# Attention in a hybrid decoder layer: three visits of TensorE per head pair instead of eight short ones

## The chip, the cores and the metric

The kernel runs on one core of a Trainium2 chip. A core has a matrix engine, TensorE (PE in the profile, with its weight loads listed apart as PEld), and three engines for elementwise work: VectorE (DVE), ScalarE (ACT) and GpSimd (POOL). SyncE (SP) issues the transfers here. All of them run their own instruction lists and meet at semaphores. The metric is device time in microseconds (us) from the start to the end of one execution; the time of a kernel is the median of its runs.

## The reference

One decoder layer on 512 tokens of width 1024, in fp32. Three sub-layers follow one another, each behind an RMS norm that is scaled and shifted by a conditioning vector:

```
x += 0.5 * (1 + ga1) * swiglu(norm1(x))          # 1024 -> 2816 -> 1024
x += (1 + ga2) * mixer(norm2(x))
x += 0.5 * (1 + ga3) * swiglu(norm3(x))
mixer: q, k, v of 16 heads of 64 = h @ w_in;  out = heads @ w_o
  8 stick-breaking heads, keys before the query only:
    z = q.k / 8;  w = sigmoid(z) * product over the keys between key and query of sigmoid(-z)
  8 forgetting heads, keys up to the query:
    q, k RMS-normed per head;  p = softmax(q.k / 8 + F[query] - F[key]),  F = running sum of log sigmoid(f)
  out = weights @ v
```

## The kernel before

**Precision and tiles.** A fp32 product is made as three matmuls of split operands: high part by high part, high by low, low by high (`mm3`, lines 127 to 130). Tokens lie along the free axis, 512 wide, so that a projection of 128 output columns is eight steps (one for each 128 of the width 1024), each of three 128x512 matmuls. A weight tile is loaded by a transfer of SP into `raw`; ACT copies it to the high part `hi` (line 123) and DVE, or the engine that `prep` (line 120) is given, subtracts that to get the low part `lo` (line 124). The accumulators are PSUM banks with four tags (line 107): three banks `mm`, two `z`, two `pt`, one `o`.

**The mixer.** The heads are taken in pairs, in `ORDER`: pairs 4 to 7 are the forgetting heads (the code says fox), 0 to 3 the stick-breaking ones. The tokens are stored last first, so that block i of 128 queries sees the last 512 - 128 i columns. For each pair `project` (line 756) makes q and k. For a fox pair the accumulator goes through `norm_start` (line 770: squares `nsq`, their high part `nsh`, on POOL the low part `nsl`) and `norm_end` (line 776: two matmuls against a block of ones into an `mm` bank, the reciprocal root `nr`, the normed `nq`). `q_stack` and `k_stack` then split the normed q and k into stacked operands: `QH`, `QL`, `KS` and, for fox, `late` (shown as `k` in the profile). These pieces wait in the list `side`, and one of them is popped for each projection step.

A unit is a pair and one block of queries, 32 in all. It has three parts on PE:

- `scores` (line 830): for each head a matmul of `QH` by `KS`, and a second one with `QL` (64 rows only for stick-breaking), into `z`; for fox a bf16 matmul adds the mask. Behind it `weigh` works on the other engines. Fox: the row maximum `mx` on DVE, exp to `fw` with the row sum `sm` on ACT, the reciprocal on DVE, the scaling of `fw` on POOL. Stick-breaking: two sigmoids `keep` and `beta` on ACT, a scan to `R` on DVE, `beta` times `R` on POOL.
- `transposed` (line 879), for each head: 4 - i transposes of the weights into `pt`, then a copy `PT` on DVE or ACT.
- `values` (line 890): the products with `V` (PV), 128*64, into `o`; after the pair's last unit `heads_out` splits `o` into `oh` and `ol`.

**The order on PE** in the mixer is written out by hand. `filler` (line 936) yields projection steps: q and k of the pairs, two of the four chunks of `V`, then the output projection for three of its eight tiles as far as its inputs are there. `advance(n)` (line 968) issues such steps up to number n. The main loop (from line 976) goes over the units and puts, for unit u: its scores, steps, the transposes of unit u - 1's first head, a step, the PV of unit u - 2, steps, the transposes of unit u - 1's second head, steps. How many steps come between is set by `target(t)` (line 656), where t counts half units: 2.5 steps for each until t = 52, from there 1.125. After the last step the rest of the output projection follows.

The other engines' orders are made by a scheduler from dependencies and priorities; the weights of the attention have a priority raised by 200 (line 848). An engine takes its list strictly in order.

Of the kernel before, what the change touches and what calls it, by code (L numbers as in the profile page):

```python
# [15 lines left out]
P = 128  # L16
# [17 lines left out]
def hybrid_layer(  # L34
# [47 lines left out]
    def nm(s):  # L82
        uid[0] += 1
        return f"{s}_{uid[0]}"
# [513 lines left out]
    SIDE = 1  # L598

    V = mp.tile([P, 4, D], F32, tag="V", name="V")  # L600
    fcol = mp.tile([P, 8, 8], F32, tag="fcol", name="fcol")[:, :4, :]
    evn = [0]

    def evac(dst, src):
# [66 lines left out]
    free_sb = mconst([P, S], BF16, "free_sb")  # L671
    keep_sb = mconst([P, S], BF16, "keep_sb")
    nc.gpsimd.memset(free_sb, 0.0)
    nc.gpsimd.affine_select(
        out=free_sb[:, :P], in_=free_sb[:, :P], compare_op=ALU.is_gt, fill=1.0, base=0, pattern=[[1, P]],
        channel_multiplier=-1,
    )
    nc.gpsimd.memset(keep_sb, 1.0)
    nc.gpsimd.affine_select(
        out=keep_sb[:, :P], in_=keep_sb[:, :P], compare_op=ALU.is_gt, fill=0.0, base=0, pattern=[[-1, P]],  # L680
        channel_multiplier=1,
    )
# [4 lines left out]
    logf = mp.tile([P, 8, 8], F32, tag="logf", name="logf")[:, :4, :]  # L687
# [68 lines left out]
    def project(p, got):  # L756
        fox = p >= NPAIR
        for u in range(2):
            wt = prep(wqk[2 * p + u], D, nc.gpsimd if fox and u else None)
            b = bank("mm")  # L760
            for k in range(KD):
                lh, ll = wk(wt, k)
                mm3(b, lh, ll, h["h"][k], h["l"][k], k == 0, k == KD - 1)
                if k == KD - 1:
                    got.append(norm_start(b) if fox else b)
                yield
# [60 lines left out]
            ]  # L827
        )

    def scores(p, i):  # L830
        while p not in ready:
            side.pop(0)()
        KS, QH, QL = ST[p]
        fox = p >= NPAIR
        n = S - i * P
        nn = max(n, 256)
        zs = [bank("z") for _ in range(2)]
        qsl, ksl = slice(i * P, (i + 1) * P), slice(S - nn, S)
        for g, z in enumerate(zs):
            nc.tensor.matmul(z[:, :nn], QH[:, g, qsl], KS[:, g, ksl], start=True, stop=False)  # L840
            if fox:
                nc.tensor.matmul(z[:, :nn], QL[:, g, qsl], late[p % 2][:, g, ksl], start=False, stop=False)
                nc.tensor.matmul(z[:, nn - n : nn - n + P], ident_b, mask_fx, start=False, stop=True)
# [6 lines left out]
    def weights(p, g, i, z, n):  # L850
        with tc.high_priority(offset=200):
            return weigh(p, g, i, z, n)

    def weigh(p, g, i, z, n):
        if p >= NPAIR:
            hd = 2 * (p - NPAIR) + g
            mx = mp.tile([P, 1], F32, tag="mx", name=nm("mx"), bufs=4)
            sm = mp.tile([P, 1], F32, tag="sm", name=nm("sm"), bufs=4)
            lq = lfq[:, i, hd : hd + 1]
            nc.vector.tensor_reduce(mx, z, AX.X, ALU.max)  # L860
            nc.vector.scalar_tensor_tensor(
                out=mx, in0=mx, scalar=lq, in1=lq, op0=ALU.add, op1=ALU.subtract, reverse1=True
            )
            w = wt2k("fw")
            act(w[:, :n], z, AF.Exp, bias=mx, accum_out=sm)
            nc.vector.reciprocal(sm, sm)
            nc.gpsimd.tensor_scalar(w[:, :n], w[:, :n], sm, 0.0, op0=ALU.mult, op1=ALU.add)
            return w, n
# [4 lines left out]
        rti[0] += 1  # L873
        nc.vector.tensor_tensor_scan(
            R[:, 1:n], keep[:, : n - 1], free_sb[:, : n - 1], 1.0, op0=ALU.mult, op1=ALU.max
        )
        nc.gpsimd.tensor_tensor(beta[:, :n], beta[:, :n], R[:, :n], op=ALU.mult)
        return beta, n

    def transposed(p, g, w, n):  # L880
        pt = bank("pt")
        for j in range(n // P):
            nc.tensor.transpose(pt[:, j * P : (j + 1) * P], w[:, j * P : (j + 1) * P], ident)  # L883
        PT = mp.tile([P, S], F32, tag="PT", name=nm("PT"), bufs=4)
        if p < NPAIR:
            nc.vector.tensor_tensor(PT[:, :n], pt[:, :n], keep_sb[:, :n], op=ALU.mult)
        elif g:
            nc.scalar.copy(PT[:, :n], pt[:, :n])
        else:
            nc.vector.tensor_copy(PT[:, :n], pt[:, :n])  # L890
        return PT

    def values(p, i, pts, ob):
        n = 4 - i
        for j in range(n):
            for g in range(2):
                nc.tensor.matmul(  # L897
                    ob[g * 64 : g * 64 + 64, i * P : (i + 1) * P],
                    V[:, i + j, (2 * p + g) * 64 : (2 * p + g + 1) * 64],
                    pts[g][:, j * P : (j + 1) * P],  # L900
                    start=j == 0,
                    stop=j == n - 1,
                )

    def heads_out(p, ob):
        if p in ORDER[-2:]:
# [66 lines left out]
            if side and done[0] % SIDE == 0:  # L973
                side.pop(0)()

    units = [(p, i) for p in ORDER for i in range(4)]
    with tc.manual_schedule(engines={ENG.PE}):
        advance(36)
        ws, pts, obs = {}, {}, {}
        for u in range(len(units) + 3):  # L980
            if u < len(units):
                ws[u] = scores(*units[u])
            for g in range(2):
                advance(target(2 * u + g))
# [12 lines left out]
        acc = SumSq(tmps(mp, "wk", NWK))

# [111 lines left out]
```

## Time and profile before

| | before |
|---|---|
| median of 3 runs | 1024.78 us (1024.21 to 1025.28) |
| profiled execution | 1024.78 us, of which the span from the first to the last instruction is 1023.0 us |
| mean granted TensorE clock | 0.998 |
| busy in the span | PE 1004.3, PEld 832.3, DVE 577.4, ACT 372.0, POOL 125.3 us |
| window 410 to 450 us, where attention starts | PE busy 34.64 of 40 us, clock 0.96 |
| window 450 to 620 us, the rest of attention | PE busy 167.15 of 170 us, DVE 130.67, ACT 105.08, POOL 68.80 |
| window 700 to 1023 us, the last sub-layer | PE busy 319.47 of 323 us |

The profile gives each engine's busy time, what its idle time waited for, and a timeline of its instructions. Matmuls overlap in the array and their ends are modelled, so the busy time of PE contains pauses inside a chain of matmuls; the times from start to start show them. In a timeline row stand the start in us, the duration, engine, line, operation, output<-inputs, tile (rows*columns for PE), shapes and the number of instructions. A bracket behind it gives idle time and what ended it.

### The profile page before, as it was taken

The numbers are of one execution on the slowest core, as the hardware profiler recorded it, in microseconds if no ns is written. First come the engines' busy times: TensorE is split into PE (matmuls) and PEld (weight loads), VectorE is DVE, ScalarE is ACT, GpSimd is POOL, SyncE is SP. The second block draws the span as 40 slices with busy tenths as digits, with TensorE's granted clock in tenths as the row PEclk, the third lists the DMA queues.
The fourth block names the chain that finished last, engine by engine and source line by source line (L and its number), as shares of the span: only waits on it lengthen the run. The fifth ranks groups of instructions, "written<-read, shape, count | busy, mean of one in ns | idle before, by whom it ended". The sixth has DMA issues, their size and how long they took to land.

```text
span 1023.0 us, 13213 instructions
## 1 busy us (share of the span) xinstructions
PE 1004.3 (98%) x5164; PEld 832.3 (81%) x5164; DVE 577.4 (56%) x950; ACT 372.0 (36%) x600; POOL 125.3 (12%) x125
## 2 busy tenths in 40 slices
PE   8999999999999999989999999999999999999998
PEld 7788788888888899767787767998888888888887
DVE  6999888524333447699867675753333233333331
ACT  4343212322222335677566461543222222123320
POOL 1000000000000123345313355100000000000000
PEclk9999999999999999999999999999999999999999
DMA  7989899433332312302111112233322222332321
GB/s 299 317 298 327 323 338 334 145 91 101 103 103 86 121 51 79 116 25 68 56 63 62 48 37 62 84 103 103 103 86 100 103 87 81 115 107 86 89 80 57
DMA packets 37358, 128.88 MB, mean 126 GB/s; under 512 B 4400, under 2 KB 4656, under 8 KB 37296
## 3 DMA queue, kind: packets, MB, share of 16 engines
q1 hardware_dynamic: 35712, 125.88, 36.1%
q10 hardware_dynamic: 1584, 2.16, 0.6%
q8 instruction: 41, 0.67, 0.3%
q14 instruction: 21, 0.17, 0.0%
HBM read 125.92 MB, written 2.10 MB: 125 GB/s over the span
## 4 chain that ended last, share of the span: by engine, by line
PE 82%; DVE 9%; issue 3%; DMA 2%; ACT 2%; POOL 1%; SPq 0%; ACTq 0%; DVEq 0%; POOLq 0%
PE mm L128 10%; PE mm L129 9%; PE mm L130 9%; PE pt L129 7%; PE pt L130 7%; PE pt L128 7%; PE z L128 6%; PE z L130 6%; PE z L129 6%; PE o L897 2%; DVE junk L214 1%; PE mm L411 1%; PE pt L883 1%; DMA wm<-wmod 1%; DVE lo L124 1%
## 5 line engine op out<-in xcount | busy, mean ns | idle before, releaser
L123 ACT CAST hi<-raw 128x1024 fp32r<-128x1024 f32 (+2 forms) x154 | 158.8, 1033 | 451.0 <-PE mm L129 144.7
L124 DVE TENSOR_TENSOR lo<-raw,hi 128x1024 fp32r<-128x1024 f32 (+2 forms) x149 | 181.0, 1217 | 132.7 <-ACT hi L123 126.9
L128 PE MATMUL mm<-hh,hi 128*128 128x512 f32 (+1 forms) x464 | 183.3, 395 | 0.5 <-DVE nu L153 0.5
L129 PE MATMUL mm<-hl,hi 128*128 128x512 f32 (+1 forms) x464 | 177.8, 383 | 0.1
L130 PE MATMUL mm<-hh,lo 128*128 128x512 f32 (+1 forms) x464 | 177.9, 383 | 0.0
L129 PE MATMUL pt<-al,hi 128*128 128x512 f32 (+1 forms) x331 | 128.2, 387 | 0.6 <-DVE al L464 0.6
L128 PE MATMUL pt<-ah,hi 128*128 128x512 f32 (+1 forms) x331 | 128.2, 387 | 0.0
L130 PE MATMUL pt<-ah,lo 128*128 128x512 f32 (+1 forms) x331 | 128.1, 387 | 0.0
L130 PE MATMUL z<-hh,lo 128*128 128x512 f32 (+1 forms) x336 | 127.3, 379 | 0.0
L128 PE MATMUL z<-hh,hi 128*128 128x512 f32 (+1 forms) x336 | 127.3, 379 | 0.0
L129 PE MATMUL z<-hl,hi 128*128 128x512 f32 (+1 forms) x336 | 127.3, 379 | 0.0
L128 PEld LDWEIGHTS mm<-hh,hi 128*128 128x128 f32 x464 | 87.6, 189 | 19.7 <-issue 3.8
L130 PEld LDWEIGHTS mm<-hh,lo 128*128 128x128 f32 x464 | 87.4, 188 | 17.3
L475 DVE SCALAR_TENSOR_TENSOR x<-pt,gcol,x 128x512 f32<-128x512 f32 (+1 forms) x51 | 36.4, 713 | 114.5 <-PE pt L130 114.5
L129 PEld LDWEIGHTS mm<-hl,hi 128*128 128x128 f32 x464 | 87.6, 189 | 15.0 <-DVE hl L168 0.3
L460 DVE TENSOR_TENSOR av<-sg,z 128x512 f32<-128x512 f32 x41 | 28.1, 686 | 105.6 <-PE z L130 105.6
L214 DVE SCALAR_TENSOR_TENSOR junk<-wm,c_bc 128x1024 f32<-128x1024 f32 x56 | 68.4, 1221 | 10.0 <-DMA wm<-wmod 9.9
L129 PEld LDWEIGHTS pt<-al,hi 128*128 128x128 f32 x331 | 62.2, 188 | 13.5 <-DVE al L464 0.9
L130 PEld LDWEIGHTS z<-hh,lo 128*128 128x128 f32 x336 | 63.2, 188 | 11.9
L129 PEld LDWEIGHTS z<-hl,hi 128*128 128x128 f32 x336 | 63.2, 188 | 11.8
L128 PEld LDWEIGHTS z<-hh,hi 128*128 128x128 f32 x336 | 63.2, 188 | 11.8
L128 PEld LDWEIGHTS pt<-ah,hi 128*128 128x128 f32 x331 | 62.2, 188 | 12.9 <-ACT ah L463 0.3
(302 smaller groups left out, 1433.4 us busy)
## 6 DMA issues: line engine op xcount, KB each, us to landing
raw<-w SPq DMA_DIRECT2D x80, 512.0 KB, 3.5
wm<-wmod SPq DMA_DIRECT2D x72, 512.0 KB, 5.7
raw<-wqk SPq DMA_DIRECT2D x16, 512.0 KB, 3.5
raw<-w1d SPq DMA_DIRECT2D x16, 448.0 KB, 3.3
raw<-w2d SPq DMA_DIRECT2D x16, 448.0 KB, 3.2
raw<-w1s SPq DMA_DIRECT2D x8, 512.0 KB, 4.9
raw<-w1d SPq DMA_DIRECT2D x8, 512.0 KB, 5.4
raw<-wo SPq DMA_DIRECT2D x8, 512.0 KB, 3.4
```

The costliest lines, as they stand in the source:

```text
L123: nc.scalar.copy(hi, raw)
L124: (lo_engine or nc.vector).tensor_tensor(lo, raw, hi.bitcast(F32), op=ALU.subtract)
L128: nc.tensor.matmul(ps, lh, rh, start=first, stop=False)
L129: nc.tensor.matmul(ps, lh, rl, start=False, stop=False)
L130: nc.tensor.matmul(ps, ll, rh, start=False, stop=last)
L214: nc.vector.scalar_tensor_tensor(out=junk, in0=wm, scalar=1.0, in1=c_bc, op0=ALU.mult, op1=ALU.mult, accum_out=mods[:, i : i + 1])
L411: nc.tensor.matmul(kb[j], lh if n < 2 else ll, h["l" if n == 1 else "h"][k], start=False, stop=k == KD - 1 and n == 2)
L460: nc.vector.tensor_tensor(av, sg, ps[1], op=ALU.mult)
L475: nc.vector.scalar_tensor_tensor(out=x[e][:, sl], in0=ps[:, sl], scalar=g_col(gm)[:, e : e + 1], in1=x[e][:, sl], op0=ALU.mult, op1=ALU.add)
L883: nc.tensor.transpose(pt[:, j * P : (j + 1) * P], w[:, j * P : (j + 1) * P], ident)
L897: nc.tensor.matmul(ob[g * 64 : g * 64 + 64, i * P : (i + 1) * P], V[:, i + j, (2 * p + g) * 64 : (2 * p + g + 1) * 64], pts[g][:, j * P : ...
```

## The change

Only the mixer is edited.

- A pair is taken in three visits, `VISITS = ((0,), (1,), (3, 2))`, instead of four units; blocks 3 and 2 share one visit, one `z` bank per head (256 + 256 columns, of which 128 + 256 are used), one scan, one `pt` bank and one `PT` copy. There are 24 visits.
- In a visit all of PE's attention work stands together: the scores of visit u, the transposes of both heads of visit u - 1, the PV of visit u - 2. The projection steps come ahead of a visit, up to the new `target(v)`: 20/3 steps for each visit until v = 19.5, from there 3.
- In `scores` the fox masks come behind the other matmuls of both heads.
- `project` no longer gives POOL the low part of the fox key weights; all `lo` are made on DVE.
- Smaller edits: `free_sb` and `keep_sb`, the masks of the scan and of the stick-breaking `PT`, are 640 wide with a second triangle (two more affine selects on POOL); `mx` and `sm` share a tile (both show as `mx`); `fcol` and `logf` share a tile.

The words that came with the change also name norms in projection banks. `norm_end` is not touched: its bank is `mm` in both kernels.

```diff
@@ weights' low part
-            wt = prep(wqk[2 * p + u], D, nc.gpsimd if fox and u else None)
+            wt = prep(wqk[2 * p + u], D)
@@ pacing
-    def target(t):
-        return int(min(36 + 2.5 * t, 163 + 1.125 * (t - 52)))
+    def target(v):
+        return int(min(36 + 20 * v / 3, 163 + 3 * (v - 19.5)))
+
+    VISITS = ((0,), (1,), (3, 2))
@@ scores
-        for g, z in enumerate(zs):
-            nc.tensor.matmul(z[:, :nn], QH[:, g, qsl], KS[:, g, ksl], start=True, stop=False)
-            if fox:
-                nc.tensor.matmul(z[:, :nn], QL[:, g, qsl], late[p % 2][:, g, ksl], start=False, stop=False)
-                nc.tensor.matmul(z[:, nn - n : nn - n + P], ident_b, mask_fx, start=False, stop=True)
-        if not fox:
-            for g, z in enumerate(zs):
-                a, _ = halves(g)
-                nc.tensor.matmul(z[:, :nn], QL[a, 0, qsl], KS[a, g, ksl], start=False, stop=True)
-        return [weights(p, g, i, z[:, nn - n : nn], n) for g, z in enumerate(zs)]
+        parts, off = [], 0
+        for i in seg:
+            n = S - i * P
+            nn = max(n, 256)
+            parts.append((i, n, slice(off, off + nn), slice(i * P, (i + 1) * P), slice(S - nn, S)))
+            off += nn
+        lo = parts[0][2].stop - parts[0][1]
+
+        def mm(z, sl, w, r, **kw):
+            nc.tensor.matmul(z[:, sl], w, r, skip_group_check=len(seg) > 1, **kw)
+
         for g, z in enumerate(zs):
+            for n, (i, _, sl, qsl, ksl) in enumerate(parts):
+                mm(z, sl, QH[:, g, qsl], KS[:, g, ksl], start=n == 0, stop=False)
             if fox:
+                for i, _, sl, qsl, ksl in parts:
+                    mm(z, sl, QL[:, g, qsl], late[p % 2][:, g, ksl], start=False, stop=False)
+        if fox:
+            for z in zs:
+                for i, n, sl, _, _ in parts:
+                    mm(z, slice(sl.stop - n, sl.stop - n + P), ident_b, mask_fx, start=False, stop=True)
+        else:
+            for i, _, sl, qsl, ksl in parts:
+                for g, z in enumerate(zs):
+                    a, _ = halves(g)
+                    mm(z, sl, QL[a, 0, qsl], KS[a, g, ksl], start=False, stop=True)
...
@@ main loop
-    units = [(p, i) for p in ORDER for i in range(4)]
+    units = [(p, seg) for p in ORDER for seg in VISITS]
     with tc.manual_schedule(engines={ENG.PE}):
-        advance(36)
         ws, pts, obs = {}, {}, {}
-        for u in range(len(units) + 3):
+        for u in range(len(units) + 2):
+            advance(target(u))
             if u < len(units):
                 ws[u] = scores(*units[u])
-            for g in range(2):
-                advance(target(2 * u + g))
-                if 0 <= u - 1 < len(units):
-                    p, i = units[u - 1]
-                    pts[p, i, g] = transposed(p, g, *ws[u - 1][g])
-                if g == 0 and 0 <= u - 2 < len(units):
-                    advance(target(2 * u) + 1)
-                    p, i = units[u - 2]
...
-                    values(p, i, (pts.pop((p, i, 0)), pts.pop((p, i, 1))), obs[p])
...
+            if 0 <= u - 1 < len(units):
+                pts[u - 1] = [transposed(units[u - 1][0], g, *ws[u - 1][g]) for g in range(2)]
+            if 0 <= u - 2 < len(units):
+                p, seg = units[u - 2]
...
+                values(p, pts.pop(u - 2), obs[p])
```

In the rows that follow stand the line, the operation, output<-inputs with buffer numbers, the size (for a product of PV 64x128) and how many alike come in a row.

PE's order at the first fox pair before, from the second head's transposes of one unit (`pt`) to the scores of another (`z`, two heads) and back to the projection (`mm`):

```order
L129 MATMUL mm_3734<-hl_2857,hi_3729 128x512
L130 MATMUL mm_3734<-hh_2849,lo_3730 128x512
L883 MATMUL pt_3754<-ident,fw_3655 128x128 x4
L840 MATMUL z_3761<-KS_3529,QH_3530 128x256
L842 MATMUL z_3761<-k_600_3374,QL_3531 128x256
L843 LDWEIGHTS ident_b
L843 MATMUL z_3761<-mask_fx,ident_b 128x128
L840 MATMUL z_3762<-KS_3529,QH_3530 128x256
L842 MATMUL z_3762<-k_600_3374,QL_3531 128x256
```

The same pair now, at its second visit:

```order
L130 MATMUL mm_3711<-hh_2848,lo_3707 128x512
L848 MATMUL z_3721<-KS_3532,QH_3533 128x384
L848 MATMUL z_3721<-k_600_3377,QL_3534 128x384
L848 MATMUL z_3722<-KS_3532,QH_3533 128x384
L848 MATMUL z_3722<-k_600_3377,QL_3534 128x384
L848 LDWEIGHTS ident_b
L848 MATMUL z_3721<-mask_fx,ident_b 128x128
L848 LDWEIGHTS ident_b
L848 MATMUL z_3722<-mask_fx,ident_b 128x128
L907 MATMUL pt_3743<-ident,fw_3646 128x128 x4
L907 MATMUL pt_3750<-ident,fw_3653 128x128 x4
L128 MATMUL mm_3711<-hh_2849,hi_3706 128x512
```

The mask of the first head moved from between the two heads' scores to behind both, and the transposes of both heads follow the masks without a projection step between.

PV (`o`) before, on PE a little later, with one projection step between it and the transposes:

```order
L883 MATMUL pt_3794<-ident,fw_3695 128x128 x3
L128 MATMUL mm_3734<-hh_2853,hi_3729 128x512
L129 MATMUL mm_3734<-hl_2861,hi_3729 128x512
L130 MATMUL mm_3734<-hh_2853,lo_3730 128x512
L897 MATMUL o_3803<-PT_3746,V 64x128
L897 MATMUL o_3803<-PT_3759,V 64x128
```

PV now:

```order
L848 MATMUL z_3794<-mask_fx,ident_b 128x128
L907 MATMUL pt_3833<-ident,fw_3729 128x128 x3
L907 MATMUL pt_3839<-ident,fw_3736 128x128 x3
L923 MATMUL o_3845<-PT_3748,V 64x128
L923 MATMUL o_3845<-PT_3755,V 64x128
```

PV moved right behind the second head's transposes; it reads `PT` of the visit before.

POOL before, from the first key weights of a fox pair (`lo`) over the norms' low parts (`nsl`) to the first scaling of weights:

```order
L124 TENSOR_TENSOR lo_3429<-raw_3427,hi_3428 128x1024
L124 TENSOR_TENSOR lo_3565<-raw_3563,hi_3564 128x1024
L773 TENSOR_TENSOR nsl_3422<-nsq_3420,nsh_3421 128x512
L124 TENSOR_TENSOR lo_3730<-raw_3728,hi_3729 128x1024
L773 TENSOR_TENSOR nsl_3461<-nsq_3459,nsh_3460 128x512
L773 TENSOR_TENSOR nsl_3549<-nsq_3547,nsh_3548 128x512
L124 TENSOR_TENSOR lo_3974<-raw_3972,hi_3973 128x1024
L773 TENSOR_TENSOR nsl_3600<-nsq_3598,nsh_3599 128x512
L867 TENSOR_SCALAR fw_3647<-fw_3647,sm_3644 128x512
```

POOL now:

```order
L776 TENSOR_TENSOR nsl_3425<-nsq_3423,nsh_3424 128x512
L776 TENSOR_TENSOR nsl_3464<-nsq_3462,nsh_3463 128x512
L776 TENSOR_TENSOR nsl_3552<-nsq_3550,nsh_3551 128x512
L776 TENSOR_TENSOR nsl_3603<-nsq_3601,nsh_3602 128x512
L890 TENSOR_SCALAR fw_3646<-fw_3646,mx_3647 128x512
```

The four splits left POOL's list. Three of them stand earlier in DVE's list; the fourth stands there between the last piece of the first pair's `KS` and the first maxima.

DVE before, at that place:

```order
L808 TENSOR_TENSOR KS_3529<-nq_3458,KS_3529 64x512
L809 CAST k_600_3374<-KS_3529 64x512
L860 TENSOR_REDUCE mx_3643<-z_3635 128x1
L860 TENSOR_REDUCE mx_3651<-z_3636 128x1
L861 SCALAR_TENSOR_TENSOR mx_3643<-mx_3643,lfq 128x1
```

DVE now:

```order
L811 TENSOR_TENSOR KS_3532<-nq_3461,KS_3532 64x512
L812 CAST k_600_3377<-KS_3532 64x512
L124 TENSOR_TENSOR lo_3961<-raw_3959,hi_3960 128x1024
L884 TENSOR_REDUCE mx_3647<-z_3638 128x1
L884 TENSOR_REDUCE mx_3654<-z_3639 128x1
```

One split of 128x1024 stands in front of the maxima of the first visit.

More of the change, by code (lines that the diff above doesn't have):

```diff
@@ L600, in hybrid_layer @@
     V = mp.tile([P, 4, D], F32, tag="V", name="V")
-    fcol = mp.tile([P, 8, 8], F32, tag="fcol", name="fcol")[:, :4, :]
+    fl32 = mp.tile([P, 8, 8], F32, tag="fl32", name="fl32")
+    fcol, logf = fl32[:, :4, :], fl32[:, 4:, :]
     evn = [0]
@@ L828, in stacks, with scores @@
         )
-    def scores(p, i):
+    def scores(p, seg):
         while p not in ready:
@@ L851, in weights, with weigh @@
+        cut, at = [], 0
+        for i, n, _, _, _ in parts:
+            cut.append((i, n, at))
+            at += n
+        return [weights(p, g, cut, z[:, lo:off], at) for g, z in enumerate(zs)]
+    def weights(*args):
         with tc.high_priority(offset=200):
-            return weigh(p, g, i, z, n)
-    def weigh(p, g, i, z, n):
+            return weigh(*args)
+    def weigh(p, g, cut, z, n):
         if p >= NPAIR:
             hd = 2 * (p - NPAIR) + g
[L857 to L863, printed above, removed]
-            w = wt2k("fw")
[L865 to L868, printed above, removed]
+            w = wt2k("fw")
+            for i, m, at in cut:
+                sl = slice(at, at + m)
+                col = mp.tile([P, 2], F32, tag="mx", name=nm("mx"), bufs=8)
+                mx, sm = col[:, 0:1], col[:, 1:2]
+                lq = lfq[:, i, hd : hd + 1]
+                nc.vector.tensor_reduce(mx, z[:, sl], AX.X, ALU.max)
+                nc.vector.scalar_tensor_tensor(
+                    out=mx, in0=mx, scalar=lq, in1=lq, op0=ALU.add, op1=ALU.subtract, reverse1=True
+                )
+                act(w[:, sl], z[:, sl], AF.Exp, bias=mx, accum_out=sm)
+                nc.vector.reciprocal(sm, sm)
+                nc.gpsimd.tensor_scalar(w[:, sl], w[:, sl], sm, 0.0, op0=ALU.mult, op1=ALU.add)
+            return w, n, cut
@@ L873, in weigh, with transposed @@
         rti[0] += 1
+        f0 = 0 if len(cut) > 1 else P
         nc.vector.tensor_tensor_scan(
-            R[:, 1:n], keep[:, : n - 1], free_sb[:, : n - 1], 1.0, op0=ALU.mult, op1=ALU.max
+            R[:, 1:n], keep[:, : n - 1], free_sb[:, f0 : f0 + n - 1], 1.0, op0=ALU.mult, op1=ALU.max
         )
         nc.gpsimd.tensor_tensor(beta[:, :n], beta[:, :n], R[:, :n], op=ALU.mult)
-        return beta, n
-    def transposed(p, g, w, n):
+        return beta, n, cut
+    def transposed(p, g, w, n, cut):
         pt = bank("pt")
@@ L885, in transposed @@
         if p < NPAIR:
-            nc.vector.tensor_tensor(PT[:, :n], pt[:, :n], keep_sb[:, :n], op=ALU.mult)
+            f0 = 0 if len(cut) > 1 else P
+            nc.vector.tensor_tensor(PT[:, :n], pt[:, :n], keep_sb[:, f0 : f0 + n], op=ALU.mult)
         elif g:
@@ L890, in transposed, with values @@
             nc.vector.tensor_copy(PT[:, :n], pt[:, :n])
[L891 to L895, printed above, removed]
-            for g in range(2):
[L897 to L903, printed above, removed]
+        return PT, cut
+    def values(p, pts, ob):
+        for i, m, at in pts[0][1]:
+            n = m // P
+            for j in range(n):
+                for g in range(2):
+                    nc.tensor.matmul(
+                        ob[g * 64 : g * 64 + 64, i * P : (i + 1) * P],
+                        V[:, i + j, (2 * p + g) * 64 : (2 * p + g + 1) * 64],
+                        pts[g][0][:, at + j * P : at + (j + 1) * P],
+                        start=j == 0,
+                        stop=j == n - 1,
+                    )
     def heads_out(p, ob):
```

35 lines of the change are left out of this document (15 added, 20 removed).

## The prediction

> **What bounds the kernel now.** I read, in this order, the page's busy line, PE's waits, PE's timeline through the mixer, the other engines' timelines ahead of PE's longest wait, and the windows.
>
> ```profile
> PE 1004.3 (98%) x5164; PEld 832.3 (81%) x5164; DVE 577.4 (56%) x950; ACT 372.0 (36%) x600; POOL 125.3 (12%) x125
> ```
> ```profile
> PE z L840 <- DVE KS L808: 3.9, 1, 3.9
> ...
> PE o L897 <- ACT PT L888: 1.3, 1, 1.3
> PE mm L620 <- DVE V L607: 1.3, 1, 1.3
> ...
> PE mm L779 <- POOL nsl L773: 1.0, 1, 1.0
> ```
> PE is the bound: busy for 1004.3 of 1023.0 us. Of the waits, these four lie in the mixer, the only stage that the diff touches. So there are two ways to gain: shorter waits, and fewer pauses inside what counts as busy. The program order has the same 4952 PE instructions in both kernels, so no matmul goes away.
>
> The longest wait costs more than its length. Windows around it (length, PE busy, granted clock, DMA):
>
> ```profile
> 438.40:442.26 3.86, 0.01 (x1) 1.00 0.40 136
> 442.70:446.10 3.40, 3.40 (x10) 0.50 0.00 0
> ```
> Just after the 3.86 us of idleness the granted clock is 0.50 for 3.40 us, worth 3.40 x 0.5 = 1.7 us of PE work. It is the only such stretch that the record has inside the mixer: the waits of 1.0 and 1.3 us have none behind them.
>
> **The change part by part.**
>
> *Key weight splits from POOL to DVE* (line 759). DVE, POOL and ACT ahead of the long wait:
>
> ```profile
> 430.95 1.22 DVE L124 TENSOR_TENSOR lo<-raw,hi 128x1024 fp32r<-128x1024 f32 x1
> ...
> 432.69 0.68 DVE L794 TENSOR_TENSOR QL<-nq,QH 64x512 fp32r<-64x512 f32 x1
> ...
> 436.22 2.90 DVE L794 TENSOR_TENSOR QL<-nq,QH 64x512 fp32r<-64x512 f32 x1
> 439.15 1.38 DVE L797 CAST QH<-QH 64x512 fp32r<-64x512 f32 x1
> ...
> 441.43 0.69 DVE L808 TENSOR_TENSOR KS<-nq,KS 64x512 fp32r<-64x512 f32 x1
> ...
> 458.02 0.42 DVE L797 CAST QH<-QH 64x512 fp32r<-64x512 f32 x1
> ```
> ```profile
> 421.52 2.39 POOL L124 TENSOR_TENSOR lo<-raw,hi 128x1024 fp32r<-128x1024 f32 x1 [1.44 <-ACT hi L123]
> 423.86 2.19 POOL L773 TENSOR_TENSOR nsl<-nsq,nsh 128x512 fp32r<-128x512 f32 x1
> ...
> 436.18 2.40 POOL L124 TENSOR_TENSOR lo<-raw,hi 128x1024 fp32r<-128x1024 f32 x1 [1.06 <-ACT hi L123]
> 438.67 1.57 POOL L773 TENSOR_TENSOR nsl<-nsq,nsh 128x512 fp32r<-128x512 f32 x1
> ```
> ```profile
> 421.83 0.59 ACT L771 ACTIVATE nsh<-mm 128x512 fp32r<-128x512 f32 x1
> ...
> 425.02 0.61 ACT L728 CAST k<-fl 8x512 fp32r<-8x512 f32 x1 [1.68 <-DVE fl L725]
> 426.08 0.69 ACT L103 ACTIVATE nr<-mm,eps_t 128x512 f32<-128x512 f32 x1 [0.45 <-POOL nsl L773]
> ```
> PE waits for KS (441.43 + 0.69 = 442.12), the end of an unbroken DVE queue. In it QL takes 2.90 us, against 0.68 for the same operation at 432.69, and it lies over POOL's split of 436.18. The QH cast takes 1.38 against 0.42 and lies over POOL's nsl. With the split gone from POOL, QL falls by 2.2 us, ends before nsl starts at 438.67, and QH falls by 1.0. Further up, nsl stands behind another POOL split although nsh was done at 422.42; it then ends earlier, and nr starts when the cast of 425.02 ends (425.63 instead of 426.08): 0.4. Together KS comes 3.6 us earlier. In DVE's new order no moved split stands between nr and KS: three of the four come before, in DVE's gaps, the fourth behind the last KS. PE also loses the 1.0 us wait for nsl, but that only brings it to the scores sooner. Remaining wait about 0.3 to 0.6 us, too short to halve the clock by the waits above: 3.6 + 1.7 = 5.3 us. Bounds: 0 if the chain is not shortened; 3.9 + 1.0 + 1.7 = 6.6 if all of these waits vanish.
>
> *Fewer, longer attention stretches.* Counted in the program order, PE leaves projection matmuls for attention 90 times before, 26 times after. What a border costs is in starts, since ends are modelled: a projection matmul starts 0.23 us after the one before it (481.69 to 481.92).
>
> ```profile
> 481.13 0.49 PE L883 MATMUL pt<-ident,fw 128*128 128x128 f32 x3
> 481.37 0.48 PE L128 MATMUL mm<-hh,hi 128*128 128x512 f32 x1
> 481.69 0.39 PE L129 MATMUL mm<-hl,hi 128*128 128x512 f32 x1
> 481.92 0.40 PE L130 MATMUL mm<-hh,lo 128*128 128x512 f32 x1
> 482.24 1.09 PE L897 MATMUL o<-PT,V 128*64 128x128 f32 x16
> 483.27 0.50 PE L128 MATMUL mm<-hh,hi 128*128 128x512 f32 x1
> 483.60 0.39 PE L129 MATMUL mm<-hl,hi 128*128 128x512 f32 x1
> ...
> 491.47 0.47 PE L840 MATMUL z<-KS,QH 128*128 128x512 f32 x1
> 491.78 0.40 PE L842 MATMUL z<-k,QL 128*128 128x512 f32 x1
> 492.02 0.23 PE L843 MATMUL z<-mask_fx,ident_b 128*128 128x128 bf16 x1
> 492.06 0.47 PE L128 MATMUL mm<-hh,hi 128*128 128x512 f32 x1
> 492.38 0.39 PE L129 MATMUL mm<-hl,hi 128*128 128x512 f32 x1
> ...
> 605.53 0.50 PE L128 MATMUL mm<-oh,hi 128*128 128x512 f32 x1
> ...
> 607.90 0.60 PE L840 MATMUL z<-KS,QH 128*128 128x384 f32 x2
> ...
> 608.80 0.50 PE L128 MATMUL mm<-oh,hi 128*128 128x512 f32 x1
> 609.14 0.39 PE L129 MATMUL mm<-ol,hi 128*128 128x512 f32 x1
> ...
> 616.46 0.55 PE L883 MATMUL pt<-ident,beta 128*128 128x128 f32 x3
> 616.76 0.48 PE L840 MATMUL z<-KS,QH 128*128 128x256 f32 x2
> ```
> - PV (o): 0.32 from the matmul ahead of it (+0.09) and 0.33 for the matmul behind it (+0.10). 32 stretches become 24: 8 x 0.19 = 1.5. But 8 of the 32 ran straight into transposes, where the border is cheaper: three transposes behind PV take 0.30 (616.46 to 616.76), else 0.24 (481.13 to 481.37), +0.06 for 0.10: less 0.3. Gain 1.2.
> - Transposes (pt): the matmul behind takes 0.32, but the last transpose is short by as much (three in 0.24), so merging them gains nothing. New is PV right behind transposes, 23 times: bounds 0 (its 0.09 is paid as before) and 23 x 0.09 = 2.1 (one pause serves both). I take the border seen in the nearest row, PV next to transposes, 0.04 cheaper than next to projections: 0.9.
> - Masks (fox): the key matmul behind a mask takes 0.31 (+0.08), 16 times in the middle of scores; the masks now come together: 1.3, or 0.9 if a mask followed by a mask takes 0.06 (a quarter of 0.23) instead of 0.04. I take 1.0. The exit to projections (492.06 to 492.38, +0.09), 16 x 0.09 = 1.4, becomes 12 exits to transposes at 0 to 0.09; at 0.06, as behind PV: gain 0.7 (0.35 to 1.4).
> - Stick-breaking scores: exit 0.34 (608.80 to 609.14, +0.11), 16 x 0.11 = 1.8, becomes 12 x 0.06: gain 1.0 (0.4 to 1.8).
>
> Sum 4.8, bounds 2.9 and 7.8.
>
> [...]
>
> *Old waits.* PV waited 1.3 us for PT because the copy came only 3 matmuls ahead; now a whole visit lies between: 1.3 gained (0 to 1.3). The 1.3 us on V is kept.
>
> *New waits.* Attention's weights have about one visit of time. In the fox stretch DVE has little to spare:
>
> ```profile
> 450.00:500.00 50.00, 48.74 (x301) 37.08 (x300) 47.16 (x96) 38.34 (x81) 26.89 (x26) 1.00 0.13 43
> ```
> (length, then PE, PEld, DVE, ACT, POOL.) DVE has 2.8 us free in 50, keeps nearly all its work, gets one 1.22 us split right in front of the first visit's maxima, and PE arrives 5.3 us earlier. Behind a late maximum on DVE stand exp on ACT, the scaling on POOL, and PE's transposes. Between 0 and 5.3 (all that the start gained); I take 5.3 - 2.8 = 2.5. Near the end only 9 matmuls lie between visits:
>
> ```profile
> 607.77 3.47 POOL L877 TENSOR_TENSOR beta<-beta,R 128x512 f32<-128x512 f32 x2 [3.11 <-ACT beta L103]
> ```
> Scores whose projection matmul follows at 605.53 (start of the pair's last 128x512 visit) have their second weights at 607.77 + 3.47 = 611.24, 5.7 us later. In the new order its transposes come after 6 transposes (0.7), PV (1.0), 9 matmuls (2.1), 384-wide scores (0.9, 607.90 to 608.80) and four transposes (0.4): 5.1. So 0.6 us of waiting; it holds for two or three of the last visits, the scoreless one most: 1.5 (0 to 4).
>
> *At no cost:* two more affine selects (POOL idles there); the merged scans, PT copies and tiles (16 DVE rows fewer, off PE's path). The norms' banks, named in the change's words, are already "mm" in line 777 of before: nothing. No DMA moves.
>
> Sum: 5.3 + 4.8 + 1.3 - 2.5 - 1.5 = 7.4 us. The profiled execution took 1024.78 us, which is also the median: 1017.4.
>
> **The rivals.**
> - DVE paces the fox stretch: the 5.3 us are given back there as waits for weights, instead of 2.5, and the tail waits 2.5: 1021.2. For it: 47.16 of 50. Against: PE waited in that stretch only for PT and V.
> - The chain is not shortened (QL is long for another reason, or a split on DVE takes the room): wait and half clock stay: 1017.4 + 5.3 = 1022.7. Against: the same operation takes 0.68 without POOL beside it.
> [...]
> - Slower: DVE's strict order puts projection splits, waiting for ACT casts, ahead of the maxima in every fox visit, so that all transposes wait. It decides from 4.0 + 7.4 + 2.0 = 13.4 us of new waits, 1.1 per visit over 12; at 1.5 per visit 1.5 x 12 = 18 in place of 4.0: 1031.4. Against: that needs weights about a visit late each time.
>
> **How the numbers follow.** Forecast 0.54, with its own range 1013.5 to 1020.5; DVE paces 0.18; chain unchanged 0.10; full borders 0.10; slower 0.08. Together the bounds reach down to 1024.8 - 6.6 - 7.8 - 1.3 = 1009.1 without new waits. The range 1012 to 1023 leaves out that corner, about half of "chain unchanged" and "slower". About 0.2% (2 us) is what a measurement of this kernel can tell from no change. Faster: 0.54 + 0.10 + 0.16 + 0.03 = 0.83; same: the rest of the second and third cases, 0.09; slower 0.08.
>
> **What would show it.** Right: the wait for KS under 1 us, no half clock near 442, QL there near 0.7 us, no POOL split before the last FFN, matmuls behind masks gone from between scores, PE busy time down by about 3 to 6 us. Wrong: PE waits on transposes (for fw or beta) above 6 us in sum, or a half clock elsewhere in the mixer.

## The result: 5.5 us slower, and the profile after

The changed kernel takes 1030.24 us (median of 9 runs, 1026.04 to 1031.31) against 1024.72 us for the kernel before in the same comparisons: ratio 1.0051, 95% interval 1.0039 to 1.0062. The forecast was 1017.4 us. The profiled execution took 1030.06 us, 5.28 more than the one of before, with a span of 1028.3 us and a mean granted clock of 0.993. Below, the profiled executions of ks_nsl1 and three_apart were disturbed ones (mean clock 0.696 and 0.849), so no line of theirs is read.

The page's busy line of after:

```profile
PE 1004.4 (98%) x5164; PEld 839.5 (82%) x5164; DVE 580.9 (56%) x934; ACT 370.2 (36%) x580; POOL 110.6 (11%) x115
```

PE is as busy as before (1004.3). PE's waits inside the mixer (engine and line, what it waited for, us in sum, times, longest):

```profile
PE pt L907 <- DVE PT L915: 4.2, 2, 2.8
PE pt L907 <- POOL fw L890: 2.5, 2, 2.3
...
PE pt L907 <- ACT PT L913: 1.5, 1, 1.5
PE mm L128 <- DVE nu L153: 1.4, 1, 1.4
...
PE z L848 <- DVE KS L811: 1.0, 2, 0.7
PE z L848 <- DVE k L812: 0.8, 1, 0.8
PE pt L907 <- POOL beta L901: 0.8, 1, 0.8
```

The wait for KS has fallen from 3.9 to 1.0 us (with 0.8 more for `k`), and PV's wait for PT is gone, as forecast. New are 9.0 us at the transposes (`pt`): 4.2 + 2.5 + 1.5 + 0.8. The largest part, 5.7 us, is for PT, the copy that empties a `pt` bank for the next transposes.

Windows of after, two waits and the stretches at half clock near them (length, then busy PE, PEld, DVE, ACT, POOL, granted clock, DMA):

```profile
455.46:458.25 2.79, 0.00 (x1) 0.04 (x1) 2.73 (x4) 2.74 (x6) 2.37 (x3) 0.86 0.00 0
457.50:464.30 6.80, 6.05 (x28) 4.88 (x29) 6.55 (x14) 1.99 (x6) 2.77 (x3) 0.50 0.00 1
504.05:506.35 2.30, 0.00 (x0) 0.00 (x1) 2.30 (x4) 0.00 (x0) 2.25 (x1) 0.77 0.23 50
505.22:512.05 6.83, 5.45 (x28) 4.50 (x28) 3.62 (x10) 2.31 (x6) 2.23 (x3) 0.50 0.48 154
```

Each of the two longest waits has a half clock beside it, of 6.8 us and not 3.4 as before. PE works 6.05 + 5.45 us in them. A 128x512 matmul starts 0.43 us behind the last one there (463.04 to 463.47) and 0.23 at full clock (465.69 to 465.92), so I take that time as worth half: 5.75 us lost, an estimate. Half clock counts as busy, which is why the busy line hides the gain at the borders (the pauses where PE changes between projections and attention).

The whole stretch from the first projection of the pairs to the last step of the output projection's first part, before and after:

```profile
409.47:657.04 247.57, 239.36 (x1510) 188.68 (x1509) 182.19 (x331) 141.71 (x292) 99.77 (x91) 0.99 0.19 62
```
```profile
410.81:662.38 251.57, 237.71 (x1509) 194.96 (x1508) 182.92 (x313) 139.91 (x272) 85.25 (x80) 0.97 0.18 61
```

It is 4.0 us longer. PE idles 8.2 us before and 13.9 after (+5.7); of its busy time half clock wastes 1.7 before and 5.75 after (+4.05); what is left of busy time is 237.7 before and 232.0 after (-5.7). The other 1.3 us of the 5.28 lie ahead of this stretch (409.47 to 410.81), in code that the change does not touch.

Why PT is late: DVE and PE in after, ahead of the wait of 2.79 us.

```profile
448.41 1.04 PE L907 MATMUL pt<-ident,fw 128*128 128x128 f32 x8
...
458.25 1.51 PE L907 MATMUL pt<-ident,fw 128*128 128x128 f32 x6 [2.79 <-DVE PT L915]
```
```profile
455.13 0.96 DVE L797 TENSOR_TENSOR QL<-nq,QH 64x512 fp32r<-64x512 f32 x1
456.12 1.38 DVE L800 CAST QH<-QH 64x512 fp32r<-64x512 f32 x1
457.42 0.68 DVE L915 COPY PT<-pt 128x512 f32<-128x512 f32 x1
```

The transposes end at 449.45, yet DVE copies them out only at 457.42. Ahead of the copy in DVE's list stand, besides the maxima, pieces of the next pair's norms and q stack, which nobody waits for yet. The next visit's transposes need both `pt` banks and stop. So the first theory is: **A, order on DVE and ACT** puts the PT copies behind pieces that can wait. Rivals: **B**, the four splits moved to DVE are the load; **C**, one visit is too short whatever the order.

### The profile page after: what moved, and what is told of

Read it like the earlier page. It is cut to its first block, busy times and chain, and to the rows that moved or that the text cites. A ratio compares the mean times of both kernels' runs of the same rounds, so it can differ in the third digit from the quotient of the medians.

```text
span 1028.3 us, 13108 instructions
## 1 busy us (share of the span) xinstructions
PE 1004.4 (98%) x5164; PEld 839.5 (82%) x5164; DVE 580.9 (56%) x934; ACT 370.2 (36%) x580; POOL 110.6 (11%) x115
## 4 chain that ended last, share of the span: by engine, by line
PE 81%; DVE 11%; issue 3%; ACT 2%; DMA 2%; POOL 1%; SPq 0%; ACTq 0%; DVEq 0%; POOLq 0%
PE mm L128 10%; PE mm L129 9%; PE mm L130 9%; PE pt L129 7%; PE pt L130 7%; PE pt L128 7%; PE z L128 6%; PE z L130 6%; PE z L129 6%; PE o L923 2%; DVE junk L214 2%; PE mm L411 1%; PE pt L907 1%; DMA wm<-wmod 1%; DVE lo L124 1%
## 5 line engine op out<-in xcount | busy, mean ns | idle before, releaser
L124 DVE TENSOR_TENSOR lo<-raw,hi 128x1024 fp32r<-128x1024 f32 (+2 forms) x153 | 184.7, 1209 | 138.6 <-ACT hi L123 132.8
L128 PE MATMUL mm<-hh,hi 128*128 128x512 f32 (+1 forms) x464 | 179.7, 387 | 1.4 <-DVE nu L153 1.4
```

Source lines behind the costliest of these rows:

```text
L124: (lo_engine or nc.vector).tensor_tensor(lo, raw, hi.bitcast(F32), op=ALU.subtract)
L128: nc.tensor.matmul(ps, lh, rh, start=first, stop=False)
```

## The experiments

Times are medians, ratios are against the kernel before in the same comparison.

### pt_prio: the PT copies at the weights' priority

```diff
+        with tc.high_priority(offset=200):
             if p < NPAIR:
                 ...  # the three forms of the PT copy
```

> The changed kernel with one edit: the copies of the transposed weights (PT) get the priority that the weights have, so that DVE's and ACT's lists take them ahead of the next pair's q and k pieces. Theory A (order on DVE and ACT: the PT copies stand behind pieces that nobody waits for, while both pt banks are needed at the next visit): PE's waits at the transposes for PT, 5.7 us in sum, fall below 1.5 us, and the half clock that follows the wait of 2.79 us goes too (3.4 us); about 1030.2 - 4.5 - 3.4 = 1022; if the second half-clock stretch goes as well, 1018.5. Theory B (the four splits moved to DVE are the load): the same waits under other names, 1028 to 1031. Theory C (one visit is too short a time whatever the order): the waits move from PT to fw, 1028 to 1031.

1023.02 us, ratio 0.9981 (0.9971 to 0.9991). PE's waits of this kernel:

```profile
PE z L848 <- ACT fw L103: 3.6, 4, 1.7
...
PE pt L907 <- POOL beta L901: 0.8, 1, 0.8
PE pt L907 <- POOL fw L890: 0.8, 2, 0.4
```

No wait for PT is left: A holds, and 7.2 us come back for an order of copies alone. The wait for fw fell with it, from 2.5 to 0.8 us. But 3.6 us have turned into waits of the scores for exp, which frees the `z` banks: part of C. Two of them, 1.74 and 1.31 us, have a half clock of 3.4 us behind them (465.1 to 468.5); the two half clocks of after are gone. The time is 1.0 us above A's 1022.

### lo_pool: the fox key splits back on POOL

```diff
-            wt = prep(wqk[2 * p + u], D)
+            wt = prep(wqk[2 * p + u], D, nc.gpsimd if fox and u else None)
```

> The changed kernel with one part undone: the fox key weights' low parts are made on POOL again. Theory A: the PT copies still stand behind the same pieces, so the waits at the transposes stay (6 to 10 us, with half clock), and the long wait ahead of the first scores comes back (2 to 4 us): 1030 to 1036. Theory B: the waits at the transposes fall below 3 us without half clock there; with the wait ahead of the first scores back, about 1030.2 - 6 - 7 + 5 = 1022. Theory C: as A.

1036.90 us, ratio 1.0115 (1.0101 to 1.0128):

```profile
PE pt L907 <- DVE PT L915: 7.8, 2, 4.7
PE z L848 <- DVE KS L811: 3.9, 1, 3.9
PE pt L907 <- POOL fw L890: 2.5, 2, 2.3
```

B falls: with the splits off DVE the wait for PT grows, and the wait for KS is back at its old 3.9 us. The time is 0.9 us above A's range.

### before_lo: the splits on DVE, alone

```diff
-            wt = prep(wqk[2 * p + u], D, nc.gpsimd if fox and u else None)
+            wt = prep(wqk[2 * p + u], D)
```

(on the kernel before)

> The kernel before with one part of the change alone: all low parts of weights on DVE. By the prediction's first term the wait for KS falls from 3.9 to below 1 us and the half clock behind it goes: 1024.7 - 5.3 = 1019.4. Theory A and C: no new waits in the fox stretch, since PE's eight stretches are as before: 1019 to 1021. Theory B: the moved splits make DVE late in the fox stretch of this order too: new waits of 3 us and more, 1023 to 1028.

1022.34 us, ratio 0.9977 (0.9968 to 0.9986); profiled 1021.82, 2.96 less than before, not 5.3. Its waits:

```profile
PE mm L128 <- DVE nu L153: 1.4, 1, 1.4
...
PE o L897 <- ACT PT L888: 1.1, 1, 1.1
PE z L840 <- ACT fw L103: 1.0, 1, 1.0
PE z L840 <- DVE KS L808: 0.9, 2, 0.7
PE z L842 <- DVE k L809: 0.8, 1, 0.8
```

The half clock is gone. The chain's waits (KS, nsl and nu before: 3.86 + 1.02 + 0.49 = 5.4) are 0.9 + 0.8 + 1.4 = 3.1: 2.3 us and 1.7 for the clock, 4.0 together, of which 1.0 is given back at the scores, which now wait for exp. The time lies between A's range and B's, 1.3 us above the one and 0.7 below the other; no new wait of 3 us appeared, which B had asked for.

### pt_act: both fox PT copies on ACT

```diff
-        elif g:
-            nc.scalar.copy(PT[:, :n], pt[:, :n])
         else:
-            nc.vector.tensor_copy(PT[:, :n], pt[:, :n])
+            nc.scalar.copy(PT[:, :n], pt[:, :n])
```

> The changed kernel with the PT copies of both fox heads on ACT, at the old priority: it takes 24 halves of a visit, 12 copies of 0.55 to 0.68 us, from DVE. Theory A: ACT's list is not as full as DVE's there, so the two waits for DVE's PT go (4.2 us, and the half clock behind the first, 3.4 us), but ACT's own copy may come late (1.5 us now, up to 3): 1022 to 1025. Theory B: DVE is relieved by 7 us as by taking the splits away: 1018 to 1022, the waits for fw fall too. Theory C: waits turn to fw, 1027 to 1031.

1023.67 us, ratio 0.9990 (0.9977 to 1.0002), inside A's range. The waits for PT are gone here too; the scores wait 3.4 us for exp in four places and the transposes 1.4 us for fw. Taking 12 copies off DVE brought no more than reordering them.

### prio_ks and prio_ks_nsl: operations of POOL that lie beside DVE's

```diff
# prio_ks, on pt_prio
-            eng = nc.vector if p == ORDER[0] else nc.gpsimd
+            eng = nc.vector
# prio_ks_nsl, also
-        nc.gpsimd.tensor_tensor(sl, sq, sh.bitcast(F32), op=ALU.subtract)
+        nc.vector.tensor_tensor(sl, sq, sh.bitcast(F32), op=ALU.subtract)
```

> The kernel of pt_prio with one more edit: the low parts of the fox keys' KS of all pairs are made on DVE (0.69 us each at the first pair) instead of POOL (2.77 us for two). In pt_prio DVE's casts beside POOL's KS and nsl took 1.39 to 1.40 us, where the same casts took 0.42 alone, and PE waited 3.6 us in four places for exp to free the z banks. Theory D (POOL beside DVE stretches DVE's casts, and that makes the maxima late): DVE gains 1.0 us for each of two or three casts per pair and pays 1.4, the z waits fall below 2 us: 1021 to 1022, about 1.5 under pt_prio. Rival E (DVE's list is simply too long for 5.3 us per visit, and two more entries per pair make it longer): z waits of 4 to 6 us, 1023.5 to 1026.

> As prio_ks, and the norms' low parts nsl on DVE too (an entry of about 0.7 us) instead of POOL (1.3 to 2.2 us), so that POOL only scales weights in the fox stretch. Theory D: the QH and k casts ahead of the first scores fall to 0.42 as well, so the 1.8 us of waits for KS and k at the first scores fall by about 1: 1020 to 1021. Rival E: DVE's list grows by two more entries per pair, z waits of 4 us and more, 1024 to 1027.

prio_ks: 1021.25 us, ratio 0.9959 (0.9946 to 0.9972). prio_ks_nsl: 1024.09 us, ratio 0.9998 (0.9986 to 1.0009). DVE's QH casts between 430 and 520 us in pt_prio, prio_ks and prio_ks_nsl (count, then busy us and mean ns):

```profile
L800 DVE CAST QH<-QH 64x512 fp32r<-64x512 f32 x8 | 8.0, 1006 | 0.2
```
```profile
L800 DVE CAST QH<-QH 64x512 fp32r<-64x512 f32 x8 | 5.2, 645 | 0.2
```
```profile
L800 DVE CAST QH<-QH 64x512 fp32r<-64x512 f32 x8 | 3.4, 422 | 0.2
```

D's mechanism is there: with nothing of POOL's q and k work beside them the casts take 0.42 us (means of 422, 414 and 417 ns for QH, `k` and QL in prio_ks_nsl). For the time it decides only half. Moving KS paid; moving nsl as well brought the z waits back (2.0 us in prio_ks, 3.9 in prio_ks_nsl), as E expected. The means of 1006 ns in pt_prio and 422 in prio_ks_nsl agree with one engine holding up the other; by what means, no run here shows.

### prio_pace: more time per fox visit

```diff
-        return int(min(36 + 20 * v / 3, 163 + 3 * (v - 19.5)))
+        return int(min(36 + 7 * v, 120 + 5.733 * (v - 12), 163 + 3 * (v - 19.5)))
```

(on pt_prio)

> The kernel of pt_prio with the visits of the fox pairs 7 projection steps apart instead of 6.67 (0.23 us more per visit, made up by closer stick-breaking visits). Rival E: time per visit is what DVE lacks, so the z waits (3.6 us) fall by 0.23 us for each visit that DVE is behind, 3 to 6 visits, about 1 us: 1022. Theory D: the waits come from the order of pieces beside POOL and change by less than 0.5 us in sum: 1022.5 to 1023.5.

1023.83 us, ratio 0.9985 (0.9973 to 0.9997): no gain. The scores' wait for exp fell from 3.6 to 0.6 us, and the wait of a projection for `nu` rose from 1.4 to 4.2. Both theories missed the time (1022, and 1022.5 to 1023.5). That PE met the same full list of DVE at another place is the likely reading, not one that a run shows.

### before_ks_nsl and before_prio_ks: eight stretches with the same edits

```diff
# both on before_lo; before_ks_nsl: KS and nsl on DVE; before_prio_ks: KS on DVE and
+        with tc.high_priority(offset=200):
             if p < NPAIR:
                 ...  # the three forms of the PT copy
```

> The control: the kernel before, eight stretches per pair, with the low parts of weights, of KS and of the norms all on DVE. It shows what the visits themselves are worth against an order with the same engines' work. By the traces' time without waits and half clock (from the first projection of the pairs to the last step of the output projection: 238.1 us in before_lo, 232.1 in pt_prio) the visits are worth 6 us, so that this one should be 4 to 6 us above prio_ks_nsl if the waits are alike; the waits at the first scores fall by about 1 us against before_lo: 1021 to 1022.5. Rival E: DVE too full here too, 1024 and more.

> The control for the two edits that helped: eight stretches as before, low parts of weights and of KS on DVE, and the PT copies at the weights' priority. If the three visits are worth the 4.7 us that starts show (before_lo against pt_prio, without waits), this one is 1 to 3 us above prio_ks, whose waits are longer: 1022 to 1024. If eight stretches with the same edits are as fast as prio_ks (1021), the visits themselves bring nothing that the waits do not take back.

before_ks_nsl: 1024.04 us, ratio 0.9981 (0.9972 to 0.9990); no better than before_lo, so that KS and nsl on DVE together did not pay here; this kernel leaves the PT copies at the old priority, and PE waits 3.7 us for them. before_prio_ks: 1020.42 us, ratio 0.9952 (0.9940 to 0.9964), as fast as prio_ks, which differs in the visits. So the visits show no gain in time once both orders have the same edits.

### ks_nsl1 and ks_nsl1_v: nsl on DVE for the first pair; V's copies earlier

```diff
# on prio_ks
+        (nc.vector if p == ORDER[0] else nc.gpsimd).tensor_tensor(sl, sq, ...)
# ks_nsl1_v, also
-                    with tc.high_priority(offset=150):
+                    with tc.high_priority(offset=250):
                         v_out(c, s, b)
```

> The kernel of prio_ks with the norms' low parts nsl on DVE for the first fox pair alone. In prio_ks PE still waits 1.9 us for KS and k ahead of the first scores and 1.4 us for nu; with nsl on DVE for all pairs these were 0.2 and 1.1 us, but the later pairs paid. Theory D (a short operation of DVE is stretched by a POOL operation beside it, so each piece belongs where the list is free): only the first chain gets shorter, by 1 to 1.5 us: 1020. Rival E (any entry added to DVE's list costs): 1021 to 1023.

> As ks_nsl1, and the copies of V out of its banks get a priority above the weights' (250 instead of 150). In prio_ks PE waited 1.6 and 0.5 us for these copies. If they wait behind maxima and PT copies in DVE's list, 1 to 1.5 us less than ks_nsl1: 1019; if the wait is the length of the copy itself, no difference; if the copies now hold up maxima, z waits of 1 us more.

1022.22 us, ratio 0.9960 (0.9946 to 0.9973), and 1021.14 us, ratio 0.9957 (0.9945 to 0.9970): neither differs from prio_ks. In ks_nsl1_v PE still waits 1.5 us for a copy of V, so raising its priority did not help. This kernel serves as the counterpart of before_prio_ks, since both have the clock at 1.00 throughout the mixer. The same stretch as above, first before_prio_ks, then ks_nsl1_v:

```profile
409.10:652.55 243.45, 237.68 (x1509) 187.21 (x1508) 179.91 (x339) 141.87 (x292) 85.26 (x82) 1.00 0.19 63
```
```profile
409.32:652.69 243.37, 233.50 (x1509) 190.59 (x1508) 184.56 (x321) 139.44 (x272) 73.80 (x72) 1.00 0.19 63
```

The lengths are equal. PE is busy 4.2 us less in visits and idle 9.9 us instead of 5.8. The gain at the borders is real and goes into waiting, nearly to the last tenth.

### rev: PV, transposes, scores

```diff
             if 0 <= u - 2 < len(units):
                 ...  # PV of u - 2
+            if 0 <= u - 1 < len(units):
+                ...  # transposes of u - 1
+            if u < len(units):
+                ws[u] = scores(*units[u])
```

(on prio_ks, where the last two stood first)

> The kernel of prio_ks with the order inside a visit turned round: PV of visit u - 2, transposes of u - 1, scores of u. The scores come 1.5 to 2 us later behind the exp that frees their banks, so the z waits (2.0 us) should go, while the weights have 1.5 to 2 us less until their transposes: if latency is what PE waits for, the waits for fw grow from 1.4 to 3 us or more; if DVE's throughput is, the sum of both stays near 3.4 us. By borders about the same (transposes straight before scores cost 0.11 us each less 0.08 at the end; PV before transposes 0.06 more). 1020 to 1023.

1038.03 us, ratio 1.0117 (1.0099 to 1.0134), far outside what I expected:

```profile
PE pt L907 <- POOL beta L901: 6.9, 9, 1.5
PE pt L907 <- POOL fw L890: 6.7, 8, 2.3
```

The waits for exp at the scores are gone, but the transposes wait 17 times for weights, 13.6 us, and the mixer has four half clocks of 3.4 us where prio_ks has one. So it is latency, not the sum of DVE's work alone: from its scores to its transposes a visit's weights have no 1.5 us to spare, in stick-breaking visits either.

### four_visits, split, three_apart: what in a visit costs the waits

```diff
# four_visits, on ks_nsl1_v
-    VISITS = ((0,), (1,), (3, 2))
+    VISITS = ((0,), (1,), (2,), (3,))
-        return int(min(36 + 20 * v / 3, 163 + 3 * (v - 19.5)))
+        return int(min(36 + 5 * v, 163 + 2.25 * (v - 26)))
# split, on ks_nsl1_v: between the scores and the transposes
+            advance(target(u) + 2)
# three_apart, on ks_nsl1_v: VISITS kept, the loop as before the change, with
+                advance(target(u + g / 2))
```

> The kernel of ks_nsl1_v with blocks 3 and 2 in visits of their own: four visits per pair, all of attention's work of a visit together, 5 projection steps apart. Theory F (the merged visit costs the waits: four maxima and four exps stand between its scores and the next scores, since both z banks must come free): the waits for exp at the scores (2.2 us) and for fw (1.4) fall by 2 to 3 us, and 8 more visits cost 8 borders of about 0.2 to 0.3 us: 1020 to 1021.5. Theory G (both heads' transposes and PV in one place cost the waits, whatever the blocks): the waits stay or grow with less time per visit, 1022 to 1025.

> The kernel of ks_nsl1_v with two projection steps (1.4 us) between the scores and the transposes of a visit. Theory G: the weights and PT get 1.4 us more, so the waits at the transposes (fw 1.4, beta 0.8 us) go, and 24 more borders at 0.05 to 0.11 us cost 1.2 to 2.6: 1020.5 to 1022. Theory F: the waits for exp at the scores (2.2 us) stay, since the scores stand as far apart as before.

> The kernel of ks_nsl1_v with the three units per pair kept but the old interleaving: scores, steps, the first head's transposes, a step, PV, steps, the second head's transposes, steps. Theory F: the merged unit's four exps still stand between its scores and the next, so waits for exp of about 2 us stay; PE's busy time lies between the two (more borders than ks_nsl1_v, fewer than eight stretches): 1021 to 1023. Theory G: the waits fall to those of before_prio_ks (5.8 us in the mixer), and with a third fewer borders than there it is the fastest: 1019 to 1020.

four_visits: 1030.01 us, ratio 1.0050 (1.0038 to 1.0063). split: 1020.41 us, ratio 0.9950 (0.9935 to 0.9966). three_apart: 1025.61 us, ratio 1.0005 (0.9992 to 1.0017).

The waits at the transposes and for exp in four_visits, then in split:

```profile
PE pt L907 <- POOL beta L901: 3.9, 5, 1.5
...
PE pt L907 <- POOL fw L890: 1.9, 5, 0.8
...
PE z L848 <- ACT fw L103: 0.6, 1, 0.6
```
```profile
PE z L848 <- ACT fw L103: 2.0, 1, 2.0
...
PE pt L907 <- POOL fw L890: 0.3, 1, 0.3
```

G holds for the transposes: with 5 steps instead of 6.67 from scores to transposes their waits grow (5.8 us), with two steps more they nearly vanish (0.3). F holds for the scores: their waits for exp fall from 2.2 us to 0.6 when the merged visit is taken apart (four_visits), and in split one of 2.0 us stays. Both missed in the times: four_visits is 8.5 us above F's range and 5 above G's, three_apart 2.6 above F's and 5.6 above G's. Why three_apart is slow stays open. Split came out at the lower end of G's range. The same stretch in split and four_visits:

```profile
410.37:652.37 242.00, 233.19 (x1509) 190.55 (x1508) 180.95 (x321) 139.26 (x272) 76.94 (x72) 1.00 0.19 63
```
```profile
409.46:661.23 251.77, 239.44 (x1509) 192.06 (x1508) 183.60 (x341) 141.38 (x292) 78.01 (x80) 0.99 0.19 61
```

Split has 23 stretches more than ks_nsl1_v and is not busier (233.19 to 233.50). four_visits is busy for 239.44 us, 1.7 of it lost to a half clock of 3.4 us: 237.7, as much as the eight stretches. So the 4.2 us go with the merged blocks, that is with 24 visits instead of 32, and not with standing together. The price of 1.2 to 2.6 us that the expectation put on split's borders was not paid.

## Why the prediction was wrong, point by point

**The start (5.3).** The mechanism was right: QL fell to 0.69 and the last QH to 0.42, no POOL split lies beside them, the half clock is gone. That it went is less certain than the prediction made it: in pt_act and prio_ks, where the same short waits remain (0.7, 0.85 and 0.3 us), a half clock of 3.4 us stands at this place again. The size was 4.0, or 3.0 with the wait for exp that follows (before_lo). The step that failed is "ends before nsl starts": POOL's nsl did not vanish, it moved beside other casts of the same chain, and 3.1 us of waits for KS, `k` and `nu` remained (before_lo) where the sum had left 0.3 to 0.6. DVE and POOL in after:

```profile
434.89 1.41 DVE L800 CAST QH<-QH 64x512 fp32r<-64x512 f32 x1
...
437.12 0.69 DVE L797 TENSOR_TENSOR QL<-nq,QH 64x512 fp32r<-64x512 f32 x1
437.84 0.42 DVE L800 CAST QH<-QH 64x512 fp32r<-64x512 f32 x1
...
439.88 1.38 DVE L812 CAST k<-KS 64x512 fp32r<-64x512 f32 x1
```
```profile
434.68 1.34 POOL L776 TENSOR_TENSOR nsl<-nsq,nsh 128x512 fp32r<-128x512 f32 x1 [9.49 <-ACT nsh L774]
439.57 1.41 POOL L776 TENSOR_TENSOR nsl<-nsq,nsh 128x512 fp32r<-128x512 f32 x1 [3.55 <-ACT nsh L774]
```

**The borders (4.8).** Measured 4.2 between the two kernels with full clock, and 5.7 between before and after with the half clock taken off. The sum held, but the way to it did not. It priced each change between projections and attention, and split has 23 more of them at no cost; four_visits, with PV behind transposes and the masks together, is as busy as the eight stretches. What was gained hangs on the merged blocks, so that the fit of 4.8 is in part luck. One part can be read directly, PV behind transposes. In after:

```profile
469.55 0.29 PE L848 MATMUL z<-mask_fx,ident_b 128*128 128x128 bf16 x2
469.67 0.83 PE L907 MATMUL pt<-ident,fw 128*128 128x128 f32 x6
470.43 0.88 PE L923 MATMUL o<-PT,V 128*64 128x128 f32 x12
471.23 0.50 PE L128 MATMUL mm<-hh,hi 128*128 128x512 f32 x1
```

Before, three transposes took 0.24 to the next start, but with the late matmul behind them 0.33 (481.13 to 481.69, less 0.23 for one projection matmul), 0.11 each. Six are 0.66; PV starts after 0.76. The pause of 0.10 is whole here, and it is 0.09 or more at all 23 such places of ks_nsl1_v, so that the 0.9 us put there were not had; two masks in front of transposes take 0.12 (469.55 to 469.67), with no pause behind them where the prediction had put 0.06, 12 times, so that 0.7 came back. In the list of chances, full borders (0.10) stands for a whole pause here and behind the 64-row scores. The runs show it at these 23 places; behind the 64-row scores six transposes take 0.80 to PV (548.61 to 549.41 in after), 0.04 more than the 0.76 here, where the exit to a projection had 0.11. That borders pay in full as a rule, no run shows.

**The old PT wait (1.3)** went, as forecast.

**The new waits (4.0) are the step that failed.** They measured 9.0 us at the transposes, and the half clock beside them another 5.75. Of the 9.0, 5.7 were for the PT copies, which the sum had at nothing. The prediction followed the weights (maxima, exp, scaling) and priced those at 2.5 in fox; they were 2.5, which is in part luck, since 0.8 is left of them once the PT copies come earlier (pt_prio). It took the PT copies to have "a whole visit" and never asked when the `pt` banks come back. The copies have no raised priority, and with both heads' transposes in one place both banks fall due at once; before, the heads were half a unit apart. And it knew the price of a half clock from the trace but put none behind the waits that it forecast. The order of the copies is the cause that the runs show: moving them alone took PT's waits and both of these half clocks away (pt_prio).

**The tail (1.5)** was 0.8.

**The rivals.** DVE pacing the fox stretch (0.18) named the engine but not the time (1021.2). The slower rival (1031.4, 0.08) gave nearly the measured time by another mechanism: splits ahead of the maxima, 1.1 us in each visit. lo_pool speaks against that, since the waits grew with the splits off DVE, and the waits sit in four visits. Of the signs set down, QL, the POOL splits and the half clock near 442 came true; the KS and k waits are 0.7, 0.8 and 0.3 instead of one below 1; the busy time did not fall, since half clock counts as busy; of the signs for "wrong", the half clock elsewhere came true, while the waits at the transposes for fw and beta were 3.3 us: the rest of the 9.0 was for PT, which the sign did not name.

What stays open: split, before_prio_ks and ks_nsl1_v lie within each other's intervals, so no order is shown to be best. Whether a split visit with a cure for the 2.0 us at the scores would come below 1020 was not run.

## What to carry to other kernels

Before putting PE work of one kind together, list every buffer that the stretch takes and ask when each comes back: the copy that empties a bank needs the same priority as the work that fills it. Fewer borders on PE are worth only what the other engines' latency leaves; price a new wait with the half clock that it can bring, as a risk, since the same waits brought one in some kernels and none in others (0.67 and 0.85 us: 3.4 us of it in pt_act, none in pt_prio). Compare an order with the old order under the same small edits: with the splits on DVE alone the visits cost 7.9 us (1030.24 against 1022.34 in before_lo), and with KS and the PT copies moved too the orders are alike (1021.25 and 1020.42).

## What the runs showed of the hardware

- Waits of 2.79 and 2.30 us each had 6.8 us of half clock beside them, while the wait of 3.86 us before had 3.4. Two waits of 1.45 and 1.38 us, 0.6 us apart (at 476.5 to 479.9), had none. The length of a wait does not decide it: in lo_pool the same wait of 3.86 us for KS has 6.8 us of half clock beside it (440.6 to 447.4); in pt_act waits of 0.67 and 0.85 us have 3.4 (439.7 to 443.1), and the same two in pt_prio have none. Nor is it the same from execution to execution: the nine of the changed kernel had mean clocks from 0.990 to 0.997, and the one with 0.997 was the fastest, at 1026.04 us. What starts a half clock and what ends it, no run here shows.
- Transposes of fp32 weights in a row take about 0.11 us for each further one: up to the next start 0.03, 0.13, 0.24 and 0.36 us for one to four (before, at 494.22, 488.13, 481.13 and 473.80). Their weight loads alone take as long (six in 0.64 us in after, at 469.62).
- The DVE casts of 64x512 took 0.42 us alone (after, 437.84) and up to 1.46 beside POOL's subtractions nsl and KS (after, 459.72); beside its scaling of fw they took 0.42 (after, 502.35), 0.53 and 0.61 (before, 459.05 and 495.50). Both casts shown above beside nsl end 0.28 us after it (436.30 after 436.02, 441.26 after 440.98).
